# Row sums of a Strassen-like output projection made head by head in 256 KB transfers, x rows loaded one at a time, and the sample rows finished two units earlier

## The chip, the cores and the metric

The kernel runs on one core of a Trainium2 chip. The metric is the device time of one execution in microseconds (us): the median of the runs. The profile is of one execution; its times count from the start of the span, the time from the first to the last instruction.

## What is computed

One layer of a streaming encoder, for 1024 prompt frames of one stream and for 16 new frames of each of 8 running streams ("the sample", 128 rows). D_MODEL is 2048; there are 8 stick-breaking attention heads and 8 retention heads of width 128.

```python
h = rms_norm(xp, norm_pre[l])
q_sb, k_sb, v_sb, gate_sb, q_r, k_r, v_r, gate_r = project(h, w_in[l], pos_p)
...
def merge(o_sb, o_r, gate_sb, gate_r, g_sb, g_r, w_out):
    y_sb = head_rms_norm(o_sb, g_sb, gate_sb.dtype) * jax.nn.silu(gate_sb)
    y_r = head_rms_norm(o_r, g_r, gate_r.dtype) * jax.nn.silu(gate_r)
    y = jnp.concatenate([y_sb, y_r], axis=-1)
    return jnp.einsum('bte,ed->btd', y, w_out)
...
xp = xp + rms_norm(out, norm_post[l])
```

Everything is float32. The sample goes through the same layer with its cached keys, values and states.

## The kernel before, in words

A float32 product is made of three: each operand is split into a high part (ACT copies it, L139 or L1261) and a low part (DVE subtracts, L140 or L1262), and PE multiplies high by high, high by low and low by high. Every weight block that PE takes is loaded by SP's queue (tile wr, wrt or wrx, four buffers), split by ACT and DVE (wh and wl, four buffers), and feeds twelve matmuls of 512 columns.

The prompt's 1024 rows are worked in two groups of 512: tiles 0 to 3 with the sample, then tiles 4 to 7. In a group the heads follow one another by a table, `order`, of projections (q, k, v, sg for attention, rq, rk, rv, rg for retention; x makes both kinds of values for two heads). Attention rows and retention run beside the projections as *jobs*: generators which `tick()` (L171) continues after each of a projection's matmuls, when the number of ticks that they asked for has passed. `place()` (L162) puts an instruction behind the last product in the order of its engine, by a dependency without a semaphore. All instructions are then in one fixed order on each engine, and an engine that waits holds everything behind it. An attention row makes a round trip through memory to be transposed: written at L574 (s_be), read at L581 (be), untangled by DVE at L587 (kp), and multiplied with the values at L711.

A finished head writes its gated output in transposed form to memory (s_y, L654; [0] for the first group, [1] for the second) and adds it to a running tile S1 (L658): in the second group, s_sum["S1"] gathers for each head the attention and the retention output.

The output projection follows Strassen's scheme in Winograd's form. Its operands are a11, a12, a22 (pieces of s_y) and four sums: S1, S2 (S1 and the attention rows of s_y[0]), s3 (the attention rows of s_y[0] and of s_y[1]) and s4 (S2 and the retention rows of s_y[0]). `row_sums(q)` (L1239) makes S2, s3 and s4 for half q of the heads, by DMAs on POOL's queue: for each sum a plain copy of four heads at once (1 MB, L1246), and a copy that adds (1 MB, L1248). Half 0 is started at the rk projection of head 6 in the second group and is drained before rg of head 7; half 1 is a job in unit 0 and is drained when unit 1 begins.

The projection itself is four *units* (`UNITS`, L280): for each half of the heads and each half of the columns, seven products named 1 to 7, of 48 matmuls each. The first two, 1 and 6 of unit 0, come before the tail stage. `fill` (L1251) loads an operand of 1 MB into the pair of tiles ml and mh (or s3, a22) and `cut` (L1258) splits it, at the steps that `due` lists. The operands of the first products are loaded during rg of head 7 by the table REFILL (L219): entry 2 holds what is done in that projection's eight slots, entry 3 what is done in product 1 of unit 0. SLOT 0 is a11, 1 is S2, 2 is a12, 3 is S1.

In the tail, `give` (L1375) takes each product's banks into the output tiles o (L1380 to L1384), squares them for the norm (L1387) and multiplies by norm_post (L1388). In unit 3 (`final`) three things are added. x rows (xr, 512 KB each, L1524) are loaded on POOL's queue behind products 1, 6 and 5. The sample's output, made earlier and kept in memory as s_raw, is finished in four column chunks: `finish_sample` (L1443) loads a chunk (rawc, L1451) and the sample's x (xrc, L1452), multiplies and adds on DVE (L1454, L1455) and stores (L1456), one chunk for each product; rawc and xrc have one buffer each. `scale` (L1390) multiplies the results by the norm's factor and adds x: on DVE with a store by SP (L1398, L1399), or on ACT with a store on POOL's queue that adds to a copy of x which `give_x` put into the output (L1394, L1395).

Of the kernel before, what the change touches and what calls it, by code (L numbers as in the profile page):

```python
# [9 lines left out]
F32 = mybir.dt.float32  # L10
F32R = mybir.dt.float32r
AF = mybir.ActivationFunctionType
ALU = mybir.AluOpType
# [3 lines left out]
P = 128  # L17
D = 2048
KT = D // P
H = 8  # L20
# [30 lines left out]
D_TI = (30, 34)  # L51
# [3 lines left out]
D_SO = 25  # L55
D_CS = 14
EPS = 1e-6
SCALE = 1.0 / math.sqrt(P)
# [4 lines left out]
def tile_hybrid_step(  # L63
# [135 lines left out]
    def cut_part(main, q, at, n):  # L199
# [21 lines left out]
        1: {2: (("load", 2),), 4: (("load", 3),), 6: (("split", 2),), 7: (("split", 3),)},  # L221
        2: {5: (("load", 0),), 6: (("load", 1),), 7: (("split", 0),)},
        3: {0: (("split", 1),), 1: (("load", 2),), 2: (("load", 3),)},
    }
# [182 lines left out]
    with ExitStack() as s1:  # L407
# [606 lines left out]
        class Head:  # L1014
# [52 lines left out]
            def end_rg(self, acc):  # L1067
                self.drain_last("ret")
                self.ret["rg"] = gate(acc, "rg")

            def do_ret(self):
                if self.gi == 0 or self.h % 2 or self.h == 0:
                    self.ret["rv"] = pair["r"][:, :, self.h % 2, :]
                self.ret_job = Job(ret_branch(self.gi, self.g, self.h, self.ret), D_NAT[phase[0]])
# [163 lines left out]

        def row_sums(q):  # L1239
            hs, hr = (slice(d * H + q * H // 2, d * H + (q + 1) * H // 2) for d in range(2))  # L1240
            for name, first, more in (
                ("S2", s_sum["S1"][:, hs, :], s_y[0][:, hs, :NB_TOK]),
                ("s3", s_y[0][:, hs, :NB_TOK], s_y[1][:, hs, :]),
                ("s4", s_sum["S2"][:, hs, :], s_y[0][:, hr, :NB_TOK]),
            ):
                place(nc.gpsimd.dma_start(s_sum[name][:, hs, :], first))  # L1246
                yield D_TI[1]
                place(nc.gpsimd.dma_start(s_sum[name][:, hs, :], more, accum_op=ALU.add))  # L1248
                yield D_TI[1]

        def fill(name, pair, q, queue):  # L1251
            h0, h1 = slice(q * H // 2, (q + 1) * H // 2), slice(H + q * H // 2, H + (q + 1) * H // 2)
            mix[name] = pair
            src = {"a11": s_y[0][:, h0], "a12": s_y[0][:, h1], "a22": s_y[1][:, h1]}
            src = src[name] if name in src else s_sum[name][:, h0]
            queue.dma_start(pair[1][:, :, :NB_TOK].bitcast(F32), src[:, :, :NB_TOK])
# [52 lines left out]
        for gi in range(2):  # L1309
            if gi:  # L1310
                mov = run["after"]
                load_rope(gi)
            phase[0] = gi
            heads = []
            for h in range(H):
                heads.append(Head(gi, h, last))
                last = heads[-1]
            if gi == 0:
                heads[0].ret.update(zip(("rq", "rk", "rg"), first))
            for step, h in order[gi][4 - 4 * gi :]:  # L1320
                if (gi, step, h) == (1, "rg", 2):
                    drain(ends["d"])
                    run["ys"] = Job(sample_out(mov), 2)
                if (gi, step, h) == (1, "rk", 6):
                    run["rows"] = Job(row_sums(0), 2)
                if (gi, step, h) == (1, "rg", 7):
                    drain(run["rows"])
                    drain(run["ys"])
                    drain(run["sums"])
                getattr(heads[h], "do_" + step)()  # L1330
# [26 lines left out]
    with ExitStack() as s3:  # L1357
# [43 lines left out]
        def added(t, c):  # L1401
            return c < 2 and t < 6

        xs_given = {}
        SYNC = mybir.DependencyInfo(mybir.DependencyClass.Sync, mybir.DependencyReason.DATA)
# [37 lines left out]
        def finish_sample():  # L1443
# [3 lines left out]
            for c in range(4):  # L1447
# [4 lines left out]
                place(nc.gpsimd.dma_start(xr, xs_flat[:, cs]))  # L1452
                yield
                nc.vector.tensor_tensor(raw, raw, gpost[:, cs], ALU.mult)  # L1454
                nc.vector.scalar_tensor_tensor(raw, raw, rs, xr, ALU.mult, ALU.add)  # L1455
# [6 lines left out]
        for n, (half, u, names) in enumerate(UNITS):  # L1462
            final = n == 3
            if n == 0:
                job = Job(row_sums(1), 100)
            if n == 1:
                drain(job)
            if n == 2:
                given_x = Job(give_x(), 2)
            pools = (accp, accq) if n % 2 == 0 else (accq, accp)  # L1470
            banks = {}
            for name in names:
# [33 lines left out]
                if final and name == "1":  # L1506
                    rest[0] = rest_of()
                used = USES[name]
                if name == "2":
# [8 lines left out]
                if final and name in "165":  # L1518
                    at = "165".index(name)
                    halves = [[(0, 1), (1, 1)], [(2, 1), (3, 1)]], [[(4, 1), (5, 1)], [(6, 1), (7, 1)]], [[(6, 0), (7, 0)]]  # L1520
                    for x, tokens in zip("hl", halves[at]):
                        xr = mp.tile([P, 2, 1024], F32, name="xr", tag=f"m{x}{(0, 1, 3)[at]}")
                        for j, (t, half_x) in enumerate(tokens):
                            nc.gpsimd.dma_start(xr[:, j], x_rows(t)[:, half_x * 1024 : half_x * 1024 + 1024])  # L1524
                            xrs[t, half_x] = xr[:, j]
                if final:
                    next(sample, None)
                if final and name == "6":
# [74 lines left out]
```

## Time and profile before

| what | value |
| --- | --- |
| median of 3 runs | 2340.72 us (2336.19 to 2345.64) |
| profiled execution, its own time | 2345.99 us |
| its span | 2344.3 us |
| mean granted TensorE clock | 0.991 |
| DMA traffic | 477.25 MB, mean 204 GB/s |

A row of the windows view gives a stretch, its length, each engine's busy time and number of instructions, the clock granted to TensorE (1.00 is full), the mean busy share of the 16 DMA engines, and the rate. In the timeline a row is start, duration, engine, line, operation, tiles, and in brackets how long the engine was idle before it and what ended that. In the view of waits a row is who waited for whom, the total, how often, and the longest. In the DMA view a row is tile, queue, how often, the size of one and the median time from issue to landing. PE is the matmul engine, PEld its weight loads, DVE is VectorE, ACT ScalarE, POOL GpSimd; SP only issues DMAs.

### The profile page before, as it was taken

How to read it: one execution, taken by the hardware profiler on the slowest of the kernel's cores; microseconds unless marked ns; L12 is line 12 of the kernel's file. 1: busy time of each engine (PE TensorE's matmuls, PEld its weight loads, DVE VectorE, ACT ScalarE, POOL GpSimd, SP SyncE). 2: the span in 40 equal slices, each digit the busy share in tenths (PEclk: the TensorE clock that was granted, in tenths of full speed). 3: DMA queues.
4: the chain of work that ended last, by engine and by line, in shares of the span. 5: the costliest groups of instructions: out<-in, count | busy, mean ns of one | idle time of the engine just before them, and what ended most of it. 6: DMA issues, size and time to landing. Idle time of an engine off the chain costs nothing.

```text
span 2344.3 us, 38591 instructions
## 1 busy us (share of the span) xinstructions
PE 2276.5 (97%) x13920; PEld 2016.2 (86%) x13920; DVE 1410.7 (60%) x2763; ACT 918.9 (39%) x1899; POOL 561.8 (24%) x819
## 2 busy tenths in 40 slices
PE   7999999999999999999999999999998999999994
PEld 7999999999999999998888888888887787888873
DVE  8246564556555563556667766676665556745666
ACT  6323332333333242334443444444443443544333
POOL 2123241414223241313221321122022212100011
PEclk9999999999999999999999999999999999999997
DMA  7659786877869787798968888787769757685576
GB/s 250 158 142 229 167 184 170 189 194 175 203 149 203 173 190 183 175 222 222 219 190 230 243 238 252 232 255 225 230 190 255 195 146 206 237 242 200 170 234 178
DMA packets 702000, 477.25 MB, mean 204 GB/s; under 512 B 234960, under 2 KB 633552, under 8 KB 697200
## 3 DMA queue, kind: packets, MB, share of 16 engines
q1 hardware_dynamic: 623776, 317.32, 52.0%
q0 software_dynamic: 41968, 133.87, 21.7%
q10 hardware_dynamic: 36064, 23.60, 3.4%
q8 instruction: 109, 1.79, 0.3%
q14 instruction: 83, 0.68, 0.1%
HBM read 372.94 MB, written 117.44 MB: 209 GB/s over the span
## 4 chain that ended last, share of the span: by engine, by line
PE 82%; DMA 6%; issue 5%; DVE 4%; ACT 1%; POOL 1%; SPq 0%; DVEq 0%; POOLq 0%; ACTq 0%
PE acc L314 48%; PE accn L373 11%; PE a L1285 7%; PE accx L401 4%; PE pa L711 2%; PE z L678 2%; PE sao L1209 1%; PE pd L847 1%; PE zc L782 1%; DMA ml<-s_y 1%; DMA s_s<-s_S 1%; PE rs L869 1%; DMA be<-s_bd 1%; DMA s_S<-s_S 1%; PE pS L902 1%
## 5 line engine op out<-in xcount | busy, mean ns | idle before, releaser
L314 PE MATMUL acc<-mh,wh 128*128 128x256 f32 (+2 forms) x2304 | 662.1, 340 | 2.8 <-DVE rv L1162 1.8
L314 PE MATMUL acc<-ml,wh 128*128 128x256 f32 (+2 forms) x2304 | 662.8, 340 | 0.8 <-DVE p0u L152 0.8
L314 PE MATMUL acc<-mh,wl 128*128 128x256 f32 (+2 forms) x2304 | 663.5, 340 | 0.0
L140 DVE TENSOR_TENSOR wl<-wr,wh 128x512 fp32r<-128x512 f32 x432 | 296.3, 689 | 427.7 <-ACT wh L139 419.8
L139 ACT ACTIVATE wh<-wr 128x512 fp32r<-128x512 f32 x432 | 272.2, 632 | 588.1 <-PE acc L314 342.9
L314 PEld LDWEIGHTS acc<-mh,wh 128*128 128x128 f32 x2304 | 422.5, 188 | 39.5 <-issue 6.6
L314 PEld LDWEIGHTS acc<-mh,wl 128*128 128x128 f32 x2304 | 422.2, 189 | 36.7 <-issue 8.2
L314 PEld LDWEIGHTS acc<-ml,wh 128*128 128x128 f32 x2304 | 422.2, 188 | 35.9 <-issue 6.6
L763 POOL DMA_DIRECT2D kc<-cache_sb_k x256 | 167.1, 658 | 282.8 <-DVE kcT L794 130.2
L373 PE MATMUL accn<-whn,mh 128*128 128x256 f32 x768 | 223.9, 292 | 0.0
L373 PE MATMUL accn<-wln,mh 128*128 128x256 f32 x768 | 217.1, 283 | 0.0
L373 PE MATMUL accn<-whn,ml 128*128 128x256 f32 x768 | 217.0, 283 | 0.0
L373 PEld LDWEIGHTS accn<-whn,mh 128*128 128x128 f32 x768 | 146.7, 191 | 9.8 <-issue 7.9
L373 PEld LDWEIGHTS accn<-wln,mh 128*128 128x128 f32 x768 | 146.7, 191 | 0.3
L373 PEld LDWEIGHTS accn<-whn,ml 128*128 128x128 f32 x768 | 146.5, 191 | 0.0
L615 DVE TENSOR_TENSOR_SCAN kp<-kp 128x640 f32<-128x640 f32 (+6 forms) x72 | 108.4, 1505 | 37.0 <-POOL kp L604 34.4
L1285 PE MATMUL a<-wh,mh 128*128 128x512 f32 x320 | 124.7, 390 | 2.4 <-DVE o L1384 2.4
L1285 PE MATMUL a<-wl,mh 128*128 128x512 f32 x320 | 125.1, 391 | 1.7 <-DVE wl L140 1.7
L1285 PE MATMUL a<-wh,ml 128*128 128x512 f32 x320 | 125.1, 391 | 0.0
L587 DVE STREAM_TRANSPOSE kp<-be 128x640 f32<-128x640 f32 (+6 forms) x72 | 95.4, 1325 | 8.0 <-DMA be<-s_bd 6.0
L140 DVE TENSOR_TENSOR wln<-wrn,whn 128x512 fp32r<-128x512 f32 x80 | 54.9, 689 | 68.1 <-ACT whn L139 65.2
L139 ACT ACTIVATE whn<-wrn 128x512 fp32r<-128x512 f32 x80 | 50.6, 632 | 115.3 <-PE acc L314 59.2
(268 smaller groups left out, 3588.5 us busy)
## 6 DMA issues: line engine op xcount, KB each, us to landing
wr<-w_in SPq DMA_DIRECT2D x384, 256.0 KB, 4.6
vc<-cache_sb_v SPq DMA_DIRECT2D x64, 512.0 KB, 7.3
wr<-w_out SPq DMA_DIRECT2D x112, 256.0 KB, 4.0
wrn<-w_in SPq DMA_DIRECT2D x80, 256.0 KB, 3.8
kc<-cache_sb_k SPq DMA_DIRECT2D x256, 64.0 KB, 4.3
kc<-cache_sb_k POOLq DMA_DIRECT2D x256, 64.0 KB, 4.6
tr<-w_out SPq DMA_DIRECT2D x32, 512.0 KB, 6.5
s_t<-ts POOLq DMA_DIRECT2D x16, 1024.0 KB, 6.4
```

Of the source, the lines that this page charges most:

```text
L139: nc.scalar.activation(hi, src, AF.Copy)
L140: nc.vector.tensor_tensor(lo, src, hi.bitcast(F32), ALU.subtract)
L314: last = nc.tensor.matmul(a[:, :m], lhs[:, j, :], rhs[w][:, j, o : o + m], start=(w == 0 and j == 0 and n == 0), stop=(w == KT // WQ - 1 a ...
L373: product[0] = nc.tensor.matmul(a, lhs[q][:, jj, ts], rhs[:, j, :], start=(w == 0 and j == 0 and n == 0 and t % 2 == 0), stop=(w == KT // ...
L401: product[0] = nc.tensor.matmul(banks[t], lhs[q][:, j, ts], rhs, start=(k == 0 and n == 0), stop=(k == KT - 1 and n == 2))
L587: place(nc.vector.transpose(dst.rearrange("p (k b j) -> p k j b", j=4, b=32), raw))
L615: nc.vector.tensor_tensor_scan(rev, rev, rev, 1.0, ALU.mult, ALU.bypass)
L678: mm = nc.tensor.matmul(z[:, :c], q2[a][:, i * P : (i + 1) * P], k2[b][:, :c], start=(m == 0), stop=(m == 2))
L711: nc.tensor.matmul(po[:, :P], at[:, j, :], rest["vn"][:, j, :], start=(j == 0), stop=(j == t))
L763: (nc.gpsimd if i < 2 else nc.sync).dma_start(kc[32 * i : 32 * i + 32, :].rearrange("p (k d) -> p k d", d=32), cache_k[0, 2 * c + j, s * 5 ...
L782: mm = nc.tensor.matmul(z[r, :], qp[:, j, r], ready[2 * j + c // 2][:, c % 2, :], start=(j == 0), stop=(j == 1),)
L1285: product[0] = nc.tensor.matmul(bank, a[:, k, ts], b, start=(name in "125" and k == 0 and n == 0), stop=(k == H // 2 - 1 and n == 2), skip ...
```

## The change

Five edits. `row_sums` makes every transfer for one head (256 KB) and waits D_RS ticks behind each: 36 in half 0, 12 in half 1. Half 0 is started at the k projection of head 4 rather than at rk of head 6, and a head's transfer waits until both branches of that head have been written (`ended`). Half 1 is drained when unit 2 begins. The split of a11 moves from slot 7 of rg's table into product 1's first slot. x rows are loaded by a job, one in 11 ticks. The sample's chunks are made in units 1 and 2, with two products rather than one between load and use.

```diff
+D_RS = (36, 12)
...
-        2: {5: (("load", 0),), 6: (("load", 1),), 7: (("split", 0),)},
-        3: {0: (("split", 1),), 1: (("load", 2),), 2: (("load", 3),)},
+        2: {5: (("load", 0),), 6: (("load", 1),)},
+        3: {0: (("split", 0),), 1: (("split", 1), ("load", 2)), 2: (("load", 3),)},
...
+            def ended(self):
+                return all("end" in x and x["end"].done for x in (self.rest, self.ret))
...
-        def row_sums(q):
-            hs, hr = (slice(d * H + q * H // 2, d * H + (q + 1) * H // 2) for d in range(2))
+        def row_sums(q, wait):
+            heads = range(q * H // 2, (q + 1) * H // 2)
             for name, first, more in (
-                ("S2", s_sum["S1"][:, hs, :], s_y[0][:, hs, :NB_TOK]),
-                ("s3", s_y[0][:, hs, :NB_TOK], s_y[1][:, hs, :]),
-                ("s4", s_sum["S2"][:, hs, :], s_y[0][:, hr, :NB_TOK]),
+                ("S2", lambda h: s_sum["S1"][:, h, :], lambda h: s_y[0][:, h, :NB_TOK]),
+                ("s3", lambda h: s_y[0][:, h, :NB_TOK], lambda h: s_y[1][:, h, :]),
+                ("s4", lambda h: s_sum["S2"][:, h, :], lambda h: s_y[0][:, H + h, :NB_TOK]),
             ):
-                place(nc.gpsimd.dma_start(s_sum[name][:, hs, :], first))
-                yield D_TI[1]
-                place(nc.gpsimd.dma_start(s_sum[name][:, hs, :], more, accum_op=ALU.add))
-                yield D_TI[1]
+                for act, src in ((nc.gpsimd.dma_start, first), (add_rows, more)):
+                    for h in heads:
+                        while not ready[h]():
+                            yield 3
+                        place(act(s_sum[name][:, h, :], src(h)))
+                        yield wait
...
-                if (gi, step, h) == (1, "rk", 6):
-                    run["rows"] = Job(row_sums(0), 2)
+                if (gi, step, h) == (1, "k", 4):
+                    run["rows"] = Job(row_sums(0, D_RS[0]), 2)
...
+        def load_x(tiles, q):
+            halves = [[(4 * q, 1), (4 * q + 1, 1)], [(4 * q + 2, 1), (4 * q + 3, 1)]] if q < 3 else [[(6, 0), (7, 0)]]
+            for xr, tokens in zip(tiles, halves):
+                for j, (t, right) in enumerate(tokens):
+                    place(nc.gpsimd.dma_start(xr[:, j], x_rows(t)[:, right * 1024 : right * 1024 + 1024]))
+                    xrs[t, right] = xr[:, j]
+                    yield 11
...
                 place(nc.gpsimd.dma_start(xr, xs_flat[:, cs]))
                 yield
+                yield
                 nc.vector.tensor_tensor(raw, raw, gpost[:, cs], ALU.mult)
...
             if n == 0:
-                job = Job(row_sums(1), 100)
-            if n == 1:
+                job = Job(row_sums(1, D_RS[1]), 100)
+            if n == 2:
                 drain(job)
-            if n == 2:
                 given_x = Job(give_x(), 2)
...
+                if n in (1, 2):
+                    next(sample, None)
...
-                    at = "165".index(name)
-                    halves = [[(0, 1), (1, 1)], [(2, 1), (3, 1)]], [[(4, 1), (5, 1)], [(6, 1), (7, 1)]], [[(6, 0), (7, 0)]]
-                    for x, tokens in zip("hl", halves[at]):
-                        xr = mp.tile([P, 2, 1024], F32, name="xr", tag=f"m{x}{(0, 1, 3)[at]}")
-                        for j, (t, half_x) in enumerate(tokens):
-                            nc.gpsimd.dma_start(xr[:, j], x_rows(t)[:, half_x * 1024 : half_x * 1024 + 1024])
-                            xrs[t, half_x] = xr[:, j]
-                if final:
-                    next(sample, None)
+                    q = (0, 1, 3)["165".index(name)]
+                    Job(load_x([mp.tile([P, 2, 1024], F32, name="xr", tag=f"m{x}{q}") for x in "hl"], q), 2)
```

The changed kernel has other line numbers: its sums are L1254 (copy) and L1262 (add), fills L1270, sample loads L1474 and L1475, its DVE lines L1478 and L1479, its store L1480.

The first place is POOL's order in the second group, from the sample's third chunk (s_raw) to head 6's attention rows. s_be and be are the round trip of a row, s_S and s_s the sums. Before:

```order
L1216 DMA s_raw<-raw 128x512
L1246 DMA s_S_109<-s_S_108 128x2048
L574 DMA s_be_6_19666<-be 128x28x32
L581 DMA be<-s_be_5_19534 128x6x128
L604 AFFINE_SELECT kp<-kp 128x128
L604 AFFINE_SELECT be<-be 128x128
L1248 DMA s_S_109<-s_y_104 128x4x512
L581 DMA be<-s_be_6_19666 128x7x128
L574 DMA s_rk_6_19813<-rk 128x16x32
L1246 DMA s_s_110<-s_y_104 128x4x512
L1248 DMA s_s_110<-s_y_105 128x2048
L1246 DMA s_s_111<-s_S_109 128x2048
```

And now, from the same row on:

```order
L1220 DMA s_raw<-raw 128x512
L1254 DMA s_s_111<-s_S_109 128x512
L575 DMA s_be_6_19682<-be 128x28x32
L582 DMA be<-s_be_5_19550 128x6x128
L1254 DMA s_s_111<-s_S_109 128x512
L605 AFFINE_SELECT kp<-kp 128x128
L605 AFFINE_SELECT be<-be 128x128
L582 DMA be<-s_be_6_19682 128x7x128
L1254 DMA s_s_111<-s_S_109 128x512
L575 DMA s_rk_6_19830<-rk 128x16x32
L1254 DMA s_s_111<-s_S_109 128x512
L1262 DMA s_s_111<-s_y_104 128x512
```

Where five transfers of 1 MB stood there are now five or six of 256 KB, the last of the three sums; the other eighteen stand earlier, the first behind the store of s_t ahead of head 4's key rows. The two last adds follow after head 6's first attention row.

The second place is POOL's queue in unit 1, from the fill of a11 (ml<-s_y) to that of S1 (ml<-s_S_108). Before:

```order
L1256 DMA ml_21435<-s_y_104 128x4x512
L1256 DMA ml_21601<-s_s_111 128x4x512
L1256 DMA ml_21474<-s_S_109 128x4x512
L1256 DMA ml_21633<-s_S_108 128x4x512
L1256 DMA s3l<-s_s_110 128x2048
```

And now:

```order
L1270 DMA ml_21453<-s_y_104 128x4x512
L1254 DMA s_s_111<-s_S_109 128x512 x3
L1480 DMA out<-rawc 128x512
L1254 DMA s_s_111<-s_S_109 128x512
L1270 DMA ml_21619<-s_s_111 128x4x512
L1262 DMA s_s_111<-s_y_104 128x512 x4
L1474 DMA rawc<-s_raw 128x512
L1475 DMA xrc<-x_sample 128x512
L1270 DMA ml_21492<-s_S_109 128x4x512
L1480 DMA out<-rawc 128x512
L1270 DMA ml_21651<-s_S_108 128x4x512
```

Between the fills now stand the last sum of half 1 and the sample's first chunks.

The third place is DVE's order in unit 3, around the end of product 3 (o_3 are output tiles of the last column quarter). Before:

```order
L1454 TENSOR_TENSOR rawc<-rawc,gpost 128x512
L140 TENSOR_TENSOR wl_23924<-wr_23921,wh_23923 128x512
L1455 SCALAR_TENSOR_TENSOR rawc<-rawc,smpr,xrc 128x512
L140 TENSOR_TENSOR wl_23963<-wrt,wh_23962 128x512
L140 TENSOR_TENSOR wl_23969<-wrt,wh_23968 128x512
L1454 TENSOR_TENSOR rawc<-rawc,gpost 128x512
L1384 TENSOR_TENSOR o_3_21845<-a_23773,o_3_21845 128x512
```

And now:

```order
L141 TENSOR_TENSOR wl_23964<-wr_23961,wh_23963 128x512
L141 TENSOR_TENSOR wl_24000<-wrt,wh_23999 128x512
L141 TENSOR_TENSOR wl_24006<-wrt,wh_24005 128x512
L141 TENSOR_TENSOR wl_24012<-wrt,wh_24011 128x512
L1399 TENSOR_TENSOR o_3_21863<-a_23815,o_3_21863 128x512
```

The sample's rows are gone from here, and one weight block more is split ahead of the output rows. On ACT and DVE the rows around the split of a11 are the same in both programs.

More of the change, by code (lines that the diff above doesn't have):

```diff
@@ L1237, in column_sums, with add_rows @@
                     yield 2 * D_CS
-        def row_sums(q):
-            hs, hr = (slice(d * H + q * H // 2, d * H + (q + 1) * H // 2) for d in range(2))
+        def row_sums(q, wait):
+            heads = range(q * H // 2, (q + 1) * H // 2)
             for name, first, more in (
-                ("S2", s_sum["S1"][:, hs, :], s_y[0][:, hs, :NB_TOK]),
-                ("s3", s_y[0][:, hs, :NB_TOK], s_y[1][:, hs, :]),
-                ("s4", s_sum["S2"][:, hs, :], s_y[0][:, hr, :NB_TOK]),
-            ):
-                place(nc.gpsimd.dma_start(s_sum[name][:, hs, :], first))
-                yield D_TI[1]
-                place(nc.gpsimd.dma_start(s_sum[name][:, hs, :], more, accum_op=ALU.add))
-                yield D_TI[1]
+                ("S2", lambda h: s_sum["S1"][:, h, :], lambda h: s_y[0][:, h, :NB_TOK]),
+                ("s3", lambda h: s_y[0][:, h, :NB_TOK], lambda h: s_y[1][:, h, :]),
+                ("s4", lambda h: s_sum["S2"][:, h, :], lambda h: s_y[0][:, H + h, :NB_TOK]),
+            ):
+                for act, src in ((nc.gpsimd.dma_start, first), (add_rows, more)):
[4 more added lines that the diff above has]
+                        yield wait
+                made.add((name, q))
+        made = set()
+        ready = {}
+        def add_rows(dst, src):
+            return nc.gpsimd.dma_start(dst, src, accum_op=ALU.add)
         def fill(name, pair, q, queue):
@@ L1253, in fill @@
             mix[name] = pair
+            assert name not in ("S2", "s3", "s4") or (name, q) in made
             src = {"a11": s_y[0][:, h0], "a12": s_y[0][:, h1], "a22": s_y[1][:, h1]}
@@ L1316, in tile_hybrid_step @@
                 heads.append(Head(gi, h, last))
+                ready[h] = heads[-1].ended
                 last = heads[-1]
```

## The prediction

> **What bounds the kernel now.** I began with the page: its busy times, then the granted clock by stretches, then who PE waited for, then the engines and queues around each wait.
>
> ```profile
> span 2344.3 us, 38591 instructions
> PE 2276.5 (97%) x13920; PEld 2016.2 (86%) x13920; DVE 1410.7 (60%) x2763; ACT 918.9 (39%) x1899; POOL 561.8 (24%) x819
> ```
>
> TensorE is busy for all but 68 us of the span, and the change takes no matmul away. It can gain only where PE stands still, where its clock is halved behind a standstill, and in the tail behind the last matmul. The stretches below hold the waits in the part that the change touches, then the three half-clock stretches behind them.
>
> ```profile
> core 0: us, PE busy (x) PEld busy (x) DVE busy (x) ACT busy (x) POOL busy (x), PEclk, DMA share, GB/s
> 1790.00:1850.00 60.00, 52.04 (x229) 41.06 (x228) 27.70 (x46) 21.63 (x43) 9.00 (x14) 0.94 0.82 215
> 1976.00:1992.00 16.00, 10.33 (x43) 8.60 (x42) 9.29 (x16) 7.29 (x14) 0.00 (x0) 0.79 0.79 212
> 2030.00:2100.00 70.00, 69.66 (x305) 56.85 (x304) 33.58 (x52) 30.14 (x47) 9.42 (x12) 1.00 0.88 276
> 2270.00:2322.00 52.00, 42.52 (x171) 33.25 (x169) 34.24 (x72) 21.19 (x47) 12.61 (x17) 0.93 0.62 180
> 2322.00:2344.30 22.30, 0.00 (x0) 0.00 (x0) 8.55 (x19) 1.62 (x6) 1.73 (x2) 0.56 0.98 258
> ...
> 1799.04:1805.87 6.83, 3.85 (x15) 3.56 (x16) 2.35 (x2) 0.54 (x1) 0.00 (x0) 0.50 0.99 258
> 1983.36:1990.19 6.83, 5.43 (x16) 4.56 (x17) 5.81 (x11) 4.21 (x10) 0.00 (x0) 0.50 0.78 264
> 2297.39:2304.20 6.81, 5.36 (x13) 4.20 (x14) 4.66 (x11) 1.93 (x6) 0.55 (x1) 0.50 0.35 116
> ```
>
> Three places lose time. A (1790 to 1850): 60 - 52.04 = 7.96 us idle, and 3.85 us of matmuls at half clock, which full clock would do in half: 1.9 us. Together 9.9. B (1976 to 1992): 5.67 idle and 2.7, together 8.4. C (2270 to 2322): 9.5 idle and 2.7, then 22.3 us without a matmul at a DMA share of 0.98. The row from 2030 gives the pace elsewhere: 305 matmuls in 69.66 us, 0.23 each. One weight block feeds twelve, 2.7 us; four blocks are buffered, so PE lives 11 us without a new one.
>
> Who ended the waits, from 1600 on:
>
> ```profile
> PE a L1285 <- DVE wl L140: 6.4, 4, 4.4
> PE pa L711 <- DVE kp L587: 6.0, 2, 5.2
> PE pa L887 <- DVE sc L871: 5.7, 1, 5.7
> PE a L1285 <- DVE o L1384: 2.4, 1, 2.4
> PE a L1285 <- DVE o L1382: 2.3, 1, 2.3
> ```
>
> **Part 1, the first half's sums (place A).** They were six transfers of 1 MB between 1764 and 1841. ACT's and DVE's rows there, then the transfers issued in 1764 to 1840, then those in 1700 to 1760:
>
> ```profile
> 1789.95 0.63 ACT L139 ACTIVATE wh<-wr 128x512 fp32r<-128x512 f32 x1 [7.26 <-DMA wr<-w_in]
> 1798.95 0.63 ACT L139 ACTIVATE wh<-wr 128x512 fp32r<-128x512 f32 x1 [5.97 <-DMA wr<-w_in]
> 1809.14 0.63 ACT L139 ACTIVATE wh<-wr 128x512 fp32r<-128x512 f32 x1 [9.56 <-DMA wr<-w_in]
> ```
> ```profile
> wr<-w_in SPq DMA_DIRECT2D x8, 256.0 KB, 10.0
> s_S<-s_y POOLq DMA_DIRECT2D x1, 1024.0 KB, 10.5
> s_s<-s_S POOLq DMA_DIRECT2D x1, 1024.0 KB, 12.3
> ```
> ```profile
> wr<-w_in SPq DMA_DIRECT2D x17, 256.0 KB, 3.3
> ```
>
> A weight block lands in 10.0 us beside the sums and in 3.3 before them. ACT and DVE run in order, so the late block holds the transposition at L587 behind it, and PE waits 5.2 us for that. The change cuts each megabyte into four. In POOL's order the first piece now stands behind the store that went out at 1572 and the last before the attention row written at 1850:
>
> ```profile
> 1572.38 0.58 POOL L1236 DMA_DIRECT2D s_t<-ts  x1 [9.07 <-DVE rkn L973]
> 1849.98 1.46 POOL L574 DMA_DIRECT2D s_be<-be  x1 [3.70 <-DVE wlo L140]
> ```
>
> So 24 pieces fall on 278 us, one in 11.6. A quarter of 10.5 to 12.3 us is 2.6 to 3.1 us in which a weight block may be late: far inside the 11 us of cover. I take the 9.9 us of A as gone, less 1.0 for pieces that meet a round trip of the attention rows: between 9.9 gained and, if the pieces only spread the stall, nothing. Each piece costs POOL another issue; between the 0.58 and the 1.46 of these two rows, 24 make 14 to 35 us of an engine that is idle for three quarters of the span: free.
>
> The nearest price of a small sum, over the whole run:
>
> ```profile
> s_S<-sg POOLq DMA_DIRECT2D x8, 256.0 KB, 6.3
> ```
>
> Four of these are 25 us in flight against 10.5 for the megabyte, 2.4 times as long. Nobody waits for a single piece, so I charge nothing for this in the sum; it is the ground of the first rival. The Trainium skill speaks against the change here, in DMA: Bandwidth & Descriptors, section "Measured (HBM→SBUF, 128 partitions, SWDGE, issued from GpSimd)": it wants transfers batched to 1 MiB or more, and these two rows agree in direction. The same page's section "Anatomy of one DMA — SWDGE (gpsimd) path" gives each transfer a fixed 2.0 us; by that, 18 more transfers in this half would be, as an estimate, 36 us more in flight, and the sum would change only if something waited for them one by one.
>
> **Part 2, the moved split (place B).** The stall has these rows of ACT and DVE:
>
> ```profile
> 1979.33 2.00 ACT L1261 ACTIVATE mh<-ml 128x1024 fp32r<-128x1024 f32 x2 [8.16 <-DMA ml<-s_y]
> 1980.42 2.36 DVE L1262 TENSOR_TENSOR ml<-ml,mh 128x1024 fp32r<-128x1024 f32 x2 [8.40 <-ACT mh L1261]
> ```
>
> Both engines stand at the split of the first operand until its megabyte has landed, and the retention score at L871 behind it holds PE. The source moves that split behind the projections. But the two programs have the same rows of ACT, DVE, POOL and SP around it: the split still stands before the last projection's blocks. Gain 0; 8.4 if the load happens to land 6 us sooner, which nothing here causes.
>
> **Part 3, the second half's sums.** They stand in unit 0, where PE hardly waits (the row from 2030: 0.34 us). Pieces or not, there is no more than that to win, and I count nothing.
>
> **Part 4, the sample (place C).** DVE's rows, ACT's, POOL's and SP's:
>
> ```profile
> 2291.87 0.69 DVE L1454 TENSOR_TENSOR rawc<-rawc,gpost 128x512 f32<-128x512 f32 x1 [6.38 <-DMA rawc<-s_raw]
> 2301.38 0.69 DVE L1382 SCALAR_TENSOR_TENSOR o<-a,o 128x512 f32<-128x512 f32 x1 [0.71 <-PE a L1285]
> 2303.51 0.69 DVE L1382 SCALAR_TENSOR_TENSOR o<-a,o 128x512 f32<-128x512 f32 x1 [1.37 <-PE a L1285]
> 2307.41 0.69 DVE L1382 SCALAR_TENSOR_TENSOR o<-a,o 128x512 f32<-128x512 f32 x1 [0.45 <-PE a L1285]
> ```
> ```profile
> 2276.28 0.63 ACT L139 ACTIVATE wh<-wr 128x512 fp32r<-128x512 f32 x1 [5.05 <-DMA wr<-w_out]
> 2265.45 2.11 POOL L1524 DMA_DIRECT2D xr<-x_prompt  x4 [3.31 <-issue]
> 2310.36 26.38 SPq L1399 DMA_DIRECT2D out<-o  x20
> ```
>
> DVE stands 6.38 us for a sample chunk; the weight block behind it comes late and PE waits 4.4 us, then runs at half clock, and DVE waits for the slower PE 0.71 + 1.37 + 0.45 = 2.5 us. In the new order no sample row is left in unit 3. What ends the span is the stream of results: it begins at 2310.36 and takes 34 us at a DMA share of 0.98, so its end follows its start, and its start follows DVE. 6.4 + 2.5 = 8.9 us earlier. Bounds: 4.4 if only PE's wait goes, 11 if the weight load that follows it also comes sooner.
>
> Where the sample goes, in units 1 and 2, DVE has its operands two products (22 us) after their issue. One gain there: before unit 2's second product DVE now cuts a weight block ahead of the a22 operand, which covers this wait; I count 1.3.
>
> ```profile
> 2169.20 0.50 PE L1285 MATMUL a<-wl,mh 128*128 128x512 f32 x1 [1.31 <-DVE wl L140]
> ```
>
> **Part 5, x rows in pieces.** They are placed behind products by an order that no semaphore enforces. In POOL's queue nothing stands between four of them, so the burst at 2265 stays, and with it the late weight block (5.05) and PE's 2.4 us for L1384. Gain 0, at most 2.4.
>
> **The sum.** 9.9 - 1.0 + 8.9 + 1.3 = 19.1 us. The profiled execution took 2345.99 us, 1.7 around its span, and would come to 2326.9. It is 5.3 above the median of the runs shown, 2340.72 (2336.19 to 2345.64); against that median I forecast 2321.6. A difference under 0.5%, 11.7 us, can't be told from none: faster means under 2329.0, slower over 2352.4.
>
> **The rivals.**
> 1. The pieces spread the stall instead of removing it: 2.4 times as long in flight, in a stage at a DMA share near 0.8, they meet other round trips. For it: the 6.3. Against: a piece holds a block 3 us, the cover is 11. A then gives nothing; 8.9 + 1.3 remain, 2330.5. Chance 0.18.
> 2. The sample takes its stall along: a DVE wait for rawc or xrc in units 1 and 2, with half clock behind it, costs 7.1 as it did (4.4 + 2.7). 2340.7 - 19.1 + 7.1 = 2328.7. For it: the chunk still goes round POOL's one queue and one buffer. Against: 22 us of cover. Chance 0.10.
> 3. Slower: POOL's queue in unit 1. A result row that waits for DVE, and four adds, now stand ahead of the fills of S2 and S1. Today:
>
> ```profile
> 2110.19 0.75 POOL L1256 DMA_DIRECT2D ml<-s_S  x1 [10.89 <-PE a L1285]
> 2116.73 2.36 DVE L1262 TENSOR_TENSOR ml<-ml,mh 128x1024 fp32r<-128x1024 f32 x2 [2.72 <-ACT mh L1261]
> ```
>
> DVE already waits 2.72 us for this cut. If the fills land over 8 us later (11 of cover less 2.7), every cut in units 1 and 2 stops PE; four such at B's price, 8.4, are 34 us against the gain of 19: 2340.7 + 14.5 = 2355. For it: four adds of 2.6 to 3.1 are 10 to 12 us ahead of the fill. Against: they go out while the fill still waits for PE. Chance 0.05.
> 4. More than forecast: C gives 11 and the 2.4 of part 5 goes too: 9.9 + 11 + 1.3 + 2.4 = 24.6, 2316.1. Chance 0.17.
>
> **How the numbers follow.** The forecast has 0.50, at 2321.6. Under 2329.0 lie nearly all of it (0.48), rival 4 (0.17) and a third to a half of rivals 1 and 2 (0.10): 0.75. Slower by over 0.5% is most of rival 3, 0.04; the rest, 0.21, is within. The range runs from rival 4 less the 4.5 by which the fastest run shown is under the median, 2311.6, taken as 2311, to rival 1 with the same 4.5 above it, 2335; outside lie rival 3 and parts of the others.
>
> **What would show it.** Right: no PE wait of over 2 us for L587 between 1570 and 1850, weight blocks at 3 to 5 us beside the sums, no half clock there; B's 5.7 us unchanged; no DVE wait for rawc in unit 3; the result stream starting some 9 us earlier, counted from the start of unit 3, and 34 us long. Wrong: a new PE wait of over 2 us with half clock between 1570 and 1850 or in units 1 and 2; B gone; or a result stream that starts sooner and ends where it did, since DVE is the bound.

## The result, and the profile after

| | median | runs | range |
| --- | --- | --- | --- |
| before | 2345.64 us | 7 | 2336.19 to 2345.98 |
| changed | 2328.18 us | 7 | 2319.67 to 2332.63 |

The ratio is 0.993 with a 95% interval of 0.9912 to 0.9948: the change takes 17.5 us, or 0.7%, off the time (the interval is 0.5 to 0.9%). The forecast was 19.1 us less, 2321.6 us, in a range of 2311 to 2335. The sign, the size and the range hold. The sum behind them holds less well, as the profile shows. First the page's head, then the windows view of the changed kernel: place A, the two half-clock stretches, and place C with the tail.

```profile
span 2328.4 us, 38643 instructions
PE 2269.0 (97%) x13920; PEld 2014.0 (86%) x13920; DVE 1411.8 (61%) x2763; ACT 918.7 (39%) x1899; POOL 583.8 (25%) x855
```
```profile
1790.00:1850.00 60.00, 59.02 (x283) 49.27 (x283) 36.81 (x62) 24.96 (x47) 13.02 (x17) 1.00 0.82 207
1655.82:1662.65 6.83, 4.87 (x18) 4.39 (x19) 3.21 (x9) 2.54 (x8) 0.00 (x0) 0.50 0.74 212
1980.09:1986.91 6.82, 4.39 (x13) 3.76 (x14) 5.80 (x12) 4.43 (x10) 0.00 (x0) 0.50 0.85 299
2262.00:2308.00 46.00, 43.12 (x186) 34.19 (x184) 33.05 (x71) 21.45 (x48) 10.70 (x14) 1.00 0.66 190
2308.00:2328.40 20.40, 0.00 (x0) 0.00 (x0) 8.91 (x19) 1.98 (x6) 1.75 (x2) 0.58 0.98 266
```

Place A is full: 283 matmuls in the 60 us that held 229 before, at full clock, and at the same DMA share, 0.82. Place C has lost its half-clock stretch. Place B (1980) still has its own. New is a half-clock stretch at 1656. The view of waits from 1560 on says what stands ahead of it; of the changed kernel these are all the rows:

```profile
PE acc L315 <- DVE rv L1166: 7.0, 1, 7.0
PE pa L888 <- DVE sc L872: 5.1, 1, 5.1
PE a L1299 <- DVE o L1399: 1.5, 1, 1.5
PE a L1299 <- DVE o L1397: 1.3, 1, 1.3
PE pa L712 <- DVE kp L588: 1.0, 1, 1.0
PE a L1299 <- DVE wl L141: 0.7, 1, 0.7
```

The old waits for L587 (5.2, now L588: 1.0) and for the weight block in unit 3 (4.4) are gone; B's is 5.1 where it was 5.7; and PE waits 7.0 us once, for the copy of the values at L1166 at 1650.

To see where the time went, take the same instruction in both traces. ACT copies every weight block at one line, in the same order in both kernels; here are the same five copies, before and then changed.

```profile
1559.92 0.66 ACT L139 ACTIVATE wh<-wr 128x512 fp32r<-128x512 f32 x1
1690.17 0.63 ACT L139 ACTIVATE wh<-wr 128x512 fp32r<-128x512 f32 x1 [1.58 <-PE acc L314]
1775.14 0.65 ACT L139 ACTIVATE wh<-wr 128x512 fp32r<-128x512 f32 x1
1868.26 0.63 ACT L139 ACTIVATE wh<-wr 128x512 fp32r<-128x512 f32 x1 [2.09 <-PE accx L401]
2267.88 0.64 ACT L139 ACTIVATE wh<-wr 128x512 fp32r<-128x512 f32 x1 [2.09 <-PE a L1285]
```
```profile
1565.00 0.65 ACT L140 ACTIVATE wh<-wr 128x512 fp32r<-128x512 f32 x1
1700.32 0.63 ACT L140 ACTIVATE wh<-wr 128x512 fp32r<-128x512 f32 x1 [1.86 <-PE acc L315]
1785.26 0.65 ACT L140 ACTIVATE wh<-wr 128x512 fp32r<-128x512 f32 x1
1867.34 0.63 ACT L140 ACTIVATE wh<-wr 128x512 fp32r<-128x512 f32 x1 [2.09 <-PE accx L402]
2263.19 0.63 ACT L140 ACTIVATE wh<-wr 128x512 fp32r<-128x512 f32 x1 [2.09 <-PE a L1299]
```

Subtract row by row, then take the steps between the differences:

| stretch (times of before) | changed less before, at its end | step | forecast |
| --- | --- | --- | --- |
| up to 1560, ahead of the first changed instruction | +5.1 | +5.1 | 0 |
| 1560 to 1690, the first pieces | +10.2 | **+5.1** | 0 |
| 1690 to 1775 | +10.1 | 0 | 0 |
| 1775 to 1868, place A | -0.9 | **-11.0** | -8.9 |
| 1868 to 2268, B and units 0 to 2 | -4.7 | -3.8 | -1.3 |
| 2268 to the end, unit 3 and tail | -15.9 | **-11.2** | -8.9 |

The first step lies where the two programs are the same. The waits up to 1560, of before and then of the changed kernel, show PE waiting for rows of the first group:

```profile
PE pd L833 <- DVE kp L587: 1.1, 2, 0.6
```
```profile
PE pd L834 <- DVE kp L588: 5.8, 5, 2.0
```

Up to there each engine has the same instructions in the same order in both programs. The same copy stands 2.4 to 9.5 us behind that of before in all twelve profiles that hold an edit of this change, the changed kernel's two and the ten variants' below. So the time of this stretch varies by several us between profiles of the same instructions, but always to one side. There is only one profile of the kernel before, so it stays open whether that one was early by chance or whether the later kernels share a cost there. From the first changed instruction on, the trace gains 21.0 us; over the whole span it gains 15.9, and the medians differ by 17.5. In place C SP's result stream starts 10.2 us sooner (2310.36 - 2295.43 is 14.9, of which 4.7 had been gained by the start of unit 3), and lasts as long as it did, 26.4 us. From its start to the end of the span it is 33.0 us, where it was 33.9; that is the last microsecond of the 11.2.

```profile
2295.43 26.42 SPq L1414 DMA_DIRECT2D out<-o  x20
```

The new wait has its cause on POOL. These are its rows ahead of the wait, then the transfers that the DMA view lists for issues from 1642.9 to 1646, and last the same two weight loads before (1636 to 1639).

```profile
1636.36 0.56 POOL L1254 DMA_DIRECT2D s_S<-s_S  x1 [3.07 <-DMA s_S<-sg]
...
1637.16 0.92 POOL L1262 DMA_DIRECT2D s_S<-s_y  x1
1639.86 0.58 POOL L1220 DMA_DIRECT2D s_raw<-raw  x1 [1.77 <-DVE raw L1219]
1640.60 1.58 POOL L575 DMA_DIRECT2D s_be<-be  x1 [0.16 <-issue]
1642.17 0.84 POOL L582 DMA_DIRECT2D be<-s_be  x1
1643.00 0.95 POOL L1262 DMA_DIRECT2D s_S<-s_y  x1
1644.01 0.58 POOL L1240 DMA_DIRECT2D s_t<-ts  x1
1644.58 0.89 POOL L1262 DMA_DIRECT2D s_S<-s_y  x1
```
```profile
s_S<-s_y POOLq DMA_DIRECT2D x2, 256.0 KB, 11.1
wr<-w_in SPq DMA_DIRECT2D x2, 256.0 KB, 13.0
```
```profile
wr<-w_in SPq DMA_DIRECT2D x2, 256.0 KB, 8.7
```

Four pieces leave within 9 us, beside a row's round trip and a column sum of 1 MB. Their mean distance was to be 11.6 us, but a piece is tied to its place in POOL's order only, and two things follow. When something ahead holds POOL (here S1 of head 3 had to land, 3.07 us), the pieces behind it leave together. And nothing keeps a piece back until its product is done: the last of the four leaves as soon as POOL has issued what stands ahead of it, long before its time, as the run with held pieces below shows. Two weight blocks land in 13.0 us instead of 8.7, more than the 11 us of cover.

### The profile page after: what moved, and what is told of

Read it like the earlier page. It is cut to its first block, busy times and chain, and to the rows that moved or that the text cites. A ratio compares the mean times of both kernels' runs of the same rounds, so it can differ in the third digit from the quotient of the medians.

```text
span 2328.4 us, 38643 instructions
## 1 busy us (share of the span) xinstructions
PE 2269.0 (97%) x13920; PEld 2014.0 (86%) x13920; DVE 1411.8 (61%) x2763; ACT 918.7 (39%) x1899; POOL 583.8 (25%) x855
## 4 chain that ended last, share of the span: by engine, by line
PE 87%; DMA 4%; DVE 4%; issue 1%; ACT 1%; SPq 1%; POOL 0%; DVEq 0%; ACTq 0%; POOLq 0%
PE acc L315 47%; PE a L1299 11%; PE accn L374 11%; PE accx L402 4%; PE pa L712 3%; PE z L679 2%; PE sao L1213 2%; DMA be<-s_bd 2%; PE pd L848 1%; PE zc L783 1%; DVE kp L588 1%; PE rs L870 1%; PE pa L888 1%; PE pS L903 1%; PE pa L893 1%
## 5 line engine op out<-in xcount | busy, mean ns | idle before, releaser
L588 DVE STREAM_TRANSPOSE kp<-be 128x640 f32<-128x640 f32 (+6 forms) x72 | 95.3, 1324 | 11.5 <-DMA be<-s_bd 11.5
```

The source lines that it names most:

```text
L588: place(nc.vector.transpose(dst.rearrange("p (k b j) -> p k j b", j=4, b=32), raw))
```

## The experiments

Each was timed in five rounds beside the kernel before, whose median on that chip and day was 2347.96 to 2349.74 us, 2 to 4 us above the table's; so ratios are compared, and the expectations' times are to be read against 2328 for the changed kernel. An interval of a ratio is 0.0012 to 0.0021 to either side, 3 to 5 us, so differences of a few microseconds rest on the traces more than on the ratios. The changed kernel's ratio is 0.993, and 0.9916 when timed again (at the end).

**The first half's sums in 1 MB again.** Row sums of half 0 as before, the rest changed:

```diff
-                if (gi, step, h) == (1, "k", 4):
-                    run["rows"] = Job(row_sums(0, D_RS[0]), 2)
+                if (gi, step, h) == (1, "rk", 6):
+                    run["rows"] = Job(row_sums_big(0), 2)
```

> The changed kernel, except that the first half's sums are again six transfers of 1 MB, started at the rk projection of head 6; all other edits stay. Theory (the sums made both the old stall A and, in pieces that leave in groups because no semaphore spaces them, the new 7.0 us wait of PE for L1166 at 1650): the wait for the values at L712 near 1800 comes back at 4 to 6 us with half clock behind it, the wait at 1650 falls to 2 us or less; 11 back less about 7 gone is 2328 + 4 = 2332 us. Rival 1 (the wait at 1650 is chance and has nothing to do with the sums): it stays near 7 us and the time is about 2338. Rival 2 (the pieces brought nothing at all, every microsecond came from the sample): A's wait stays away and the time is 2328.

Ratio 0.9952 (0.9934 to 0.9971). Its view of waits:

```profile
PE pa L712 <- DVE kp L588: 6.7, 2, 5.8
PE acc L315 <- DVE rv L1166: 1.9, 1, 1.9
```

Against the changed kernel, by the same copies of weight blocks, it gains 6.6 us from 1565 to 1700 and loses 10.9 from 1785 to 1867; at 1946 it stands 4.5 us behind, all counted from 1565. The ratios agree: 0.9952 - 0.993 is 0.0022, 5 us (8 us against 0.9916). So the pieces make the wait at 1650, and part 1 is worth about 5 us, half of what it takes off place A. Both rivals fall.

**Size or density?** The 1 MB transfers over the long window, still begun at the k projection of head 4 and 144 ticks apart; and the pieces in the short one:

```diff
-                    run["rows"] = Job(row_sums(0, D_RS[0]), 2)
+                    run["rows"] = Job(row_sums_big(0), 2)
```
```diff
-D_RS = (36, 12)
+D_RS = (8, 12)
-                if (gi, step, h) == (1, "k", 4):
+                if (gi, step, h) == (1, "rk", 6):
```

> The changed kernel, except that the first half's sums are six transfers of 1 MB spread over the new, long window: from the k projection of head 4 (as soon as all four heads are written), 144 ticks apart, the same bytes per time as the pieces. It tells size from density. Theory (the size matters: a megabyte holds the weight blocks behind it for about 10 us, whenever it goes): weight blocks beside it land in 9 to 12 us, one or more PE waits of 2 to 6 us with half clock between 1630 and 1850; ratio 0.994 to 0.998. Rival (only the density of the old window mattered): no such wait; ratio 0.993 or less, less because the group of pieces at 1650 is gone.

> The changed kernel, except that its 24 pieces of 256 KB start at the rk projection of head 6, 8 ticks apart, so that they fall into the window of the six old transfers. Theory of size: small pieces there leave the wait at L712 near 1800 small (2 us or less), and without the group at 1650 the time is the best of all, ratio 0.990. Theory of density: the same bytes in the same 66 us delay the weight blocks as much as before, PE waits 4 to 6 us near 1800 with half clock; ratio 0.994 to 0.996.

Ratios 0.9982 (0.9969 to 0.9995) and 0.9967 (0.9956 to 0.9979). The longest waits of the first, then of the second:

```profile
PE pa L888 <- DVE sc L872: 8.9, 2, 5.1
PE acc L315 <- DVE rv L1166: 6.1, 1, 6.1
```
```profile
PE pa L712 <- DVE kp L588: 8.1, 1, 8.1
PE acc L315 <- DVE rv L1166: 3.2, 1, 3.2
```

In the first, besides the 5.1 of place B, there are three waits (6.1 at 1652, 3.8 at 1729, 2.7 at 1783); in the second one of 8.1 near 1808, longer than the old one. By the copies of weight blocks, each kernel stands 9 to 10 us behind the changed one at the start of unit 3. The answer is both. Three of the six megabytes, though 30 us and more apart, are followed within 20 us by one of these three waits, and small pieces stop PE when they are dense. Of the arrangements tried, only small and far apart costs little. Neither single theory had that; the theory of size is wrong for the second kernel, the theory of density for the first. Of the theory of size one figure missed too: over 1764 to 1840 weight blocks landed in 5.9 us (median), not in 9 to 12, as beside the pieces; right behind a megabyte single ones took 9 to 11.

**Pieces held by a semaphore.** Each piece of half 0 waits for the product that it stands behind:

```diff
-                        place(act(s_sum[name][:, h, :], src(h)))
+                        (place if q else hold)(act(s_sum[name][:, h, :], src(h)))
...
+    def hold(inst):
+        tc.add_manual_dep(inst.ins, product[0].ins.name, HELD, reason="held until a product is done")
```

> The changed kernel, except that each piece of the first half's sums waits by a semaphore for the product that it stands behind, so that pieces can't leave in groups. Theory (grouped pieces make the wait at 1650): that wait falls from 7.0 to 2 us or less and its half clock shortens; 2328 - 5 to 7 = 2321 to 2323 us. Rival 1 (holding POOL's queue delays the attention rows' round trips behind a piece): new PE waits for L712 of over 2 us between 1570 and 1850, 2332 or more. Rival 2 (the wait at 1650 comes from the rows' own transfers): it stays over 4 us, 2328.

Ratio 0.9903 (0.9885 to 0.992), 6 us less than the changed kernel's 0.993 and 3 us less than its 0.9916. Its wait, then the last two of the four pieces:

```profile
PE acc L320 <- DVE rv L1171: 3.1, 1, 3.1
```
```profile
1645.86 0.91 POOL L1267 DMA_DIRECT2D s_S<-s_y  x1 [1.07 <-PE accx L407]
1662.91 0.85 POOL L1267 DMA_DIRECT2D s_S<-s_y  x1 [15.58 <-PE acc L320]
```

The wait falls from 7.0 to 3.1, and the transposition is no longer among the waits. By the copies of weight blocks the stretch from 1560 to 1690 loses 1.7 us instead of 5.1. The group isn't gone: the first two pieces still leave 0.8 us apart (1638.13 and 1638.94), and the third 6.9 us behind them. What moves is the fourth, from 1.6 us behind the third to 17.1: in the changed kernel it had left that long before its product was done. The theory holds in sign; of the wait it explains 4 us, not 5.

**And none while values are projected.** The same, with no piece placed during a projection x:

```diff
             def do_x(self):
+                run["quiet"] = True
                 banks = project_both(mov)
+                run["quiet"] = False
...
-                        while not ready[h]():
+                        while run.get("quiet") or not ready[h]():
```

> Pieces held by a semaphore as in the run e4_pieces_held, and none of them placed while a projection of values for two heads (x) runs; the rest as changed. Theory (what was left of the wait for L1166 near 1650, 3.1 us, is the two pieces that still go out between 1638 and 1647): the wait falls to 1.9 us or less, as with the old sums; 0 to 3 us less than e4_pieces_held's ratio of 0.9903, so 0.989 to 0.990. Rival (what was left is the attention row's own round trip in small packets): the wait stays near 3 us and the ratio at 0.990.

Ratio 0.9893 (0.9872 to 0.9914).

```profile
PE acc L320 <- DVE rv L1173: 4.1, 1, 4.1
```

Here no piece leaves between 1600 and 1661, and the wait is 4.1 us. My theory falls. The rival, the row's own round trip, would fit, but no run takes the round trip out, so that it makes the rest is not shown. What is shown is the size with and without pieces. In the six profiles where pieces go by their order alone (the changed kernel twice, and the four variants that keep its first half) the wait is 6.0 to 7.4 us. In the five without a piece there it is 1.8 (before), 1.9 (the old sums), 3.2 (the short window), 4.1 (here) and 2.7 (the last version below).

**The sample late again**, with the x rows still by a job; and **sample and x rows both as before**:

```diff
-                if n in (1, 2):
-                    next(sample, None)
...
+                if final:
+                    next(sample, None)
```
```diff
-                    Job(load_x([mp.tile([P, 2, 1024], F32, name="xr", tag=f"m{x}{q}") for x in "hl"], q), 2)
+                    for _ in load_x([mp.tile([P, 2, 1024], F32, name="xr", tag=f"m{x}{q}") for x in "hl"], q):
+                        pass
```

> The changed kernel, except that the sample's four chunks are finished in unit 3 again, one product between load and use. Theory (place C was the sample's alone): a DVE wait for rawc of about 6 us and a PE wait of about 4 us for the weight block come back in unit 3, the result stream starts 9 to 11 us later; 2328 + 9 to 11 = 2337 to 2339 us. Rival (the x rows, now issued by a job, are what brought the end forward): 2330 or less.

> The changed kernel with parts 4 and 5 both undone: the sample in unit 3 and the x rows issued at once ahead of its chunks, the rest as changed. Up to here the sample late beside x rows by a job cost about 4 us (3 in the profile, from the start of unit 3), and x rows at once beside the sample early cost nothing, while the profiles of before and after differ by 11 us from the start of unit 3 on. Theory (either edit alone takes most of that stall away, since the sample's loads then no longer stand behind four x rows in POOL's queue): the DVE wait for rawc of 5 to 7 us and the PE wait of about 4 us are both there, unit 3 to the end is 9 to 12 us longer than in the changed kernel, median 2328 + 9 to 12 = 2337 to 2340 us or a ratio to before near 0.997. Rival (the 11 us were chance in the profiles): 4 us as before, ratio 0.9948.

Ratios 0.9948 (0.9931 to 0.9965) and 0.997 (0.9955 to 0.9985). From the start of unit 3 to the end the first takes 2.9 us longer than the changed kernel, the second 11.3. The second kernel's PE wait, up to 4.7 us, is the old one; the first has one of 2.1 for a weight block. Here is the second kernel's row, and then POOL's last load of a sample chunk in the second and in the first:

```profile
PE a L1299 <- DVE wl L141: 7.4, 3, 4.7
```
```profile
2288.41 0.54 POOL L1474 DMA_DIRECT2D rawc<-s_raw  x1 [3.66 <-DMA out<-rawc]
```
```profile
2273.43 0.54 POOL L1474 DMA_DIRECT2D rawc<-s_raw  x1 [4.20 <-DMA out<-rawc]
```

So my theory for the first kernel falls: 11 us need both, the sample in unit 3 and the x rows at once. With the x rows by a job, they stand on POOL behind a chunk's store and loads, and the last chunk is loaded 11.5 us sooner (15.0 by the rows, less the 3.5 by which that kernel's unit 3 starts sooner).

**Parts 1 and 4 alone.** The split, the second half's sums and the x rows as before:

```diff
-                job = Job(row_sums(1, D_RS[1]), 100)
+                job = Job(row_sums_big(1), 100)
...
-        2: {5: (("load", 0),), 6: (("load", 1),)},
+        2: {5: (("load", 0),), 6: (("load", 1),), 7: (("split", 0),)},
```

> Parts 1 and 4 alone: the first half's sums in pieces and the sample in units 1 and 2; the split of a11, the second half's sums (1 MB, drained as unit 1 begins) and the x rows are as in the kernel before. Theory (parts 2, 3 and 5 are worth nothing): 2328 us, within 2. Rival 1 (the x rows or the later drain were worth something): 2331 to 2334. Rival 2 (the pieces of the second half cost something by delaying the fills in units 0 and 1): 2325 or less.

Ratio 0.9926 (0.9911 to 0.9942), as the changed kernel, and from the start of unit 3 on it gains as much (11.0 us). Parts 2, 3 and 5 bring nothing that the runs can tell when 1 and 4 are there. With the pair above: the x rows by a job are worth 8 of C's 11 us when the sample is late (5 by the medians, 0.997 - 0.9948), and nothing when it is early.

**Place B.** The splits of a11 and S2, tied behind the last product; that of a11 is again in slot 7 of rg's table:

```diff
-                        split=lambda q: cut(SLOT[q]),
+                        split=lambda q: cut(SLOT[q], *((place,) if q < 2 else ())),
```

> The changed kernel, except that the splits of the first two operands, a11 and S2, are tied behind the last product issued (a11's in the last slot of the projection before, S2's in the second slot of product 1), so that on ACT and DVE the split of a11 now really stands behind two more weight blocks and the retention scores. Theory (place B is the split standing ahead of work that PE needs; part 2 did nothing since the source order of an untied split is not its place in the program): PE's wait for L872 near 1977 falls from 5.1 us to under 1, the half clock behind it goes, no new wait at product 1 of over 2 us; 5 + 1.7 = 5 to 7 us less, ratio 0.990 to 0.991. Rival (the late block is the weight block itself, held by SP's queue, which stood 9.4 us in issuing the second operand's load): a PE wait of 3 to 6 us remains near 1980 and the ratio stays at 0.993.

Ratio 0.9932 (0.992 to 0.9944).

```profile
PE a L1299 <- ACT mh L1275: 1.8, 1, 1.8
PE pa L888 <- DVE sc L872: 0.5, 1, 0.5
```
```profile
1972.13 8.41 SPq L1270 DMA_DIRECT2D ml<-s_S  x1
```
```profile
1987.06 0.63 ACT L140 ACTIVATE wh<-wr 128x512 fp32r<-128x512 f32 x1 [3.89 <-DMA wr<-w_out]
1987.59 1.99 ACT L1275 ACTIVATE mh<-ml 128x1024 fp32r<-128x1024 f32 x2
```

The old wait is gone (0.5 of 5.1), so the untied split was its cause. But now the split stands on ACT behind a weight block that comes late, since SP stood 8.4 us in issuing the load ahead of it, and product 1 waits 1.8 us for the split, with half clock behind. The trace gains 2.7 us between 1946 and 2038; the median can't tell that from nothing.

**All three together**, with the split one slot earlier, ahead of that late block; and the changed kernel again beside it:

```diff
-        2: {5: (("load", 0),), 6: (("load", 1),)},
-        3: {0: (("split", 0),), 1: (("split", 1), ("load", 2)), 2: (("load", 3),)},
+        2: {5: (("load", 0),), 6: (("split", 0), ("load", 1))},
+        3: {0: (("split", 1),), 1: (("load", 2),), 2: (("load", 3),)},
```

> The run e10_held_quiet with, beside that, the split of a11 tied behind the last product one slot earlier than in e9_split_placed, so that it stands ahead of the weight block that SP's queue brings late and behind the two that are there in time. Theory (in e9_split_placed the split came behind that late block, which made the new wait of 1.8 us at product 1): no PE wait over 1 us between 1975 and 1995 and no half clock there; 5 to 7 us less than e10_held_quiet, ratio 0.9865 to 0.988. Rival (the late block itself now stops PE in product 1): a wait of 2 to 4 us at product 1, ratio within 0.001 of e10_held_quiet.

> The changed kernel again, beside the two others on the same chip, as their base. Every theory: ratio 0.993, and a wait of PE for L1166 near 1650 of 6 to 7.5 us, which would show that this wait is no chance of the first profile; if it is chance, under 3 us.

The changed kernel again: 2332.17 us, ratio 0.9916 (0.9895 to 0.9937), and its wait at 1650 is there again:

```profile
PE acc L315 <- DVE rv L1166: 6.3, 1, 6.3
```

All three together: 2324.74 us, ratio 0.9891 (0.9872 to 0.991), the shortest of all. Its longest waits from 1560 on:

```profile
PE pa L898 <- DVE S L913: 2.9, 3, 1.3
PE acc L320 <- DVE rv L1173: 2.7, 1, 2.7
```

B's wait and half clock are gone; a wait of 1.3 for S at 1987 is what came in their place. Between 1946 and 2038 the trace gains 4.3 us on the changed kernel (0.6 without the tied split). The median is 7.4 us under the changed kernel's on the same chip, of which the tied split has 1.8, less than the 5 to 7 expected and less than the runs can tell from nothing. The version beats both kernels; that each of its three edits shortens the time is not shown by the medians. The traces show it for the held pieces (at 1650) and the tied split (at 1946 to 2038).

## Why the prediction came out

**Right in sign and size, with errors that cancel.** The three terms were 8.9 for A, 8.9 for C and 1.3 for the a22 cut. The trace gave 11.0, 11.2 and 1.4 (the difference falls from 3.3 to 4.7 us across that cut), so each place gained its forecast or more. Against that stand 5.1 us lost at 1650, a place which the prediction gave no term, and 5.1 ahead of the first changed instruction, whose cause is open. That the sum came within 1.6 us of the measured gain is luck. The time itself is 6.6 us above the forecast 2321.6, of which 4.9 come from the median of before: 2345.64 in seven runs, 2340.72 in the three that I had.

**The step that failed** is in part 1: "So 24 pieces fall on 278 us, one in 11.6", and from it "far inside the 11 us of cover". The mean is right, the spacing isn't: of the 24 pieces of the changed kernel five leave within 2 us of the one ahead. I had said of the x rows that they are placed "by an order that no semaphore enforces" and that their burst therefore stays; the pieces are placed by the same call, and I did not carry the sentence over. The runs show the price: 7.0 and 6.3 us of waiting with the pieces, 1.9 without, 3.1 with the pieces held. Rival 1, that the pieces spread the stall, was half right. It had the sign of the missing term, but not its mechanism: pieces don't spread a stall of their own length over the stage, they leave bunched, behind whatever holds POOL and ahead of their products. The sign that I had named for a wrong step (a new wait of over 2 us with half clock between 1570 and 1850) is the one that came.

**Place A** went as forecast, and for the reason given. The DMA view of 1764 to 1840 has weight blocks that land in 5.9 us beside the pieces, not in the 3 to 5 that I had named, but far from 10.0. That is 2.6 us more than the 3.3 ahead of the sums, as a quarter of the megabyte's time said:

```profile
wr<-w_in SPq DMA_DIRECT2D x11, 256.0 KB, 5.9
```

That a quarter of the size holds a block a quarter as long holds only if the pieces are far apart; in the old window, a quarter of the size with four times the number stopped PE for 8.1 us.

**The rule of the Trainium skill** that I weighed, batching to 1 MiB or more (DMA: Bandwidth & Descriptors, section "Measured (HBM→SBUF, 128 partitions, SWDGE, issued from GpSimd)"), would have gone against the change. The runs go against the rule for this use: the same bytes in 1 MB transfers, spread over the same window, cost 10 us more. It is a rule for the rate of a transfer, and no wait of PE shown here is for a sum; what counted was what the sums held up.

**Place C** had the right number and half of the cause. I gave all of it to the sample and called the x rows worth nothing. Each of the two edits alone takes most of it: 8 of 11 us for the x rows, all 11 for the sample. Beside the sample in its new place the x rows are indeed worth nothing, and their burst stayed, as forecast, with weight blocks that land in 8.1 us beside it (8.4 before). The bound of 11 was the better value: PE's waits for the output rows (2.4 and 2.3) fell to 1.5 and 1.3, and 22.7 us behind the last matmul became 20.5.

**Place B, part 3 and rivals 2 and 3.** B stayed, 5.1 us, as the unchanged order on ACT and DVE said. No wait for the sample reached PE in units 1 and 2, though DVE did wait once for rawc, 2.2 us. The fills weren't late enough to matter: PE's longest wait between 2030 and 2260 is 0.7 us.

## What to carry to other kernels

When background transfers must not disturb a stream of loads, make them small and keep them apart, and keep them apart with a semaphore: a place in a queue's order sets only who goes first, and the pieces leave in groups when the queue is released, or well ahead of the work that they were to follow. When two programs have the same instruction order at a stall, an edit of the source there does nothing; tie the instruction, and look what it then stands behind. When two edits remove the same stall, undo both as well as each, or the first that you undo gets the wrong credit.

## What the runs showed of the hardware

In the stretch at 1640 to 1648 of the changed kernel transfers land close to the order in which they were issued, across the queues of SP and POOL: of the twelve issued there, three pairs of neighbours changed places and no others. The two weight loads on SP's queue took 13.0 us where the sums, the round trip and a 1 MB store on POOL's queue had been issued beside them in 8 us. A small transfer is therefore not quick behind others: two adds of 256 KB took 11.1 us there (median), as much as a whole megabyte took elsewhere (10.5).

Half clock needs no long wait. A PE wait of 1.8 us was followed by 3.4 us at half clock at 1649 before and at 1989 with the tied split; others of 1.9 us (with the old sums, at 1652) and even 3.4 us (parts 1 and 4 alone, at 1974) had none. The Trainium skill, TensorE: Matmul & The Clock Gate, section "Part 1: The HAM clock gate (the "warmup" mystery)", puts the half clock behind at least one idle window of about 3.4 us, in windows that run freely. The lengths of the stretches ahead of the tail agree (3.4, 6.8 and once 10.2 us), but a wait of 1.8 us was enough here. A free-running window may be why equal waits differ, but no run here shows that.

SP can stand in the issue of one load for 9.4 us (the load of S2 at 1970 in the changed kernel; 8.4 with the tied split), right behind the write of an attention row, and the weight loads behind it wait with it.
